# A hybrid decoder layer on one core: the MLP's up projection by Strassen's seven block products

## The chip, the cores and the metric

The kernel runs on one core of a Trainium2 chip. The metric is the device time of one execution in microseconds (us); less is better. The engines named below are PE (matrix products and transposes), DVE (vector engine), ACT (scalar engine), POOL (GpSimd) and SP, which here only issues transfers. Each engine runs its own list of instructions in order and waits, instruction by instruction, for what the others produce.

## The reference

One decoder layer on 512 tokens of 1024 channels, in fp32. Two mixers (HGRN2 and native sparse attention) read the same normalised input; then come the parts that matter here:

```python
merged = (jax.nn.sigmoid(ga) * (y_a @ w_branch_a[i])
          + jax.nn.sigmoid(gb) * (y_b @ w_branch_b[i]))
h = h + rms_norm(merged @ w_out[i], norm_post_mix[i])
v = rms_norm(h, norm_pre_mlp[i])
ff = jnp.square(jax.nn.relu(v @ w_up[i])) @ w_down[i]
h = h + rms_norm(ff, norm_post_mlp[i])
e = (p[i] @ w_ple[i]) * jax.nn.sigmoid(h @ w_ple_gate[i])
h = h + rms_norm(e, norm_ple[i])
```

`w_up` is 1024 x 4096, `w_down` 4096 x 1024, the branch weights, `w_out` and `w_ple_gate` are 1024 x 1024, and `w_ple` is 256 x 1024. A projection must be nearly as exact as in fp32.

## The kernel before

**Products in three parts.** Each fp32 operand is split into a high part, which ACT makes by a cast to the reduced type fp32r, and a low part, which is the rest and which DVE makes by a subtraction (`split`, lines 60 and 61). A product is then three matmuls, high by high, high by low and low by high, added in PSUM (the accumulator banks that PE writes). The order of instructions on each engine is set by a scheduler at build time.

**Weights.** `weights` (line 89) lets SP load 512 KB into a `raw` tile of 128 x 1024, ACT cast it into `whi`, and DVE subtract for `wlo`. There are three `raw` tiles and six pairs of `whi` and `wlo` from the merge on, in two pools that take turns.

**Stages.** Up to about 685 us stand the input norm, the projections, the attention and HGRN2; their order of instructions is the same before and after. The merge (lines 824 to 868) computes 16 tiles of 128 channels, in turns of branch a and branch b, and gates them into `ta` and `tb`. `w_out` follows token tile by token tile (`proj_n`, line 886, `acc` tiles in PSUM). Its function `evac_o` (lines 924 to 941) takes each of four tiles of 128 tokens through: sum of squares (ACT, `sqs`), product with the norm's weights (DVE, `facc`), reciprocal root (`rsa` and `rsb` on DVE, `rsr` on POOL), residual with `x` into `h1` (listed as `h`; DVE), a second sum of squares and norm into `vn` (DVE), and transposes of `vn` by PE into two PSUM banks named `tr`, from which ACT and DVE make `vh` and `vl`, the operand of the up projection. `h1` stays on chip.

**MLP.** In four quarters of 1024 columns of `w_up`, the up projection has eight tiles of 128 columns each. The weights stand still in PE and 512 tokens of `vh` and `vl` move through: 8 x 3 matmuls of 512 columns for a tile. The first four tiles of quarter 0 are done in halves of 256 tokens (`up_mm`, line 963), tokens 0 to 255 first. `up_evac` applies Relu and Square (ACT) and splits into `fh` and `fl`. After each quarter `proj_n` multiplies these with 1024 rows of `w_down` into `facc`. At the end come `w_ple`, the last quarter of `w_down` with its residual, `w_ple_gate` and the output.

Of the kernel before, what the change touches and what calls it, by code (L numbers as in the profile page):

```python
# [7 lines left out]
FT = mybir.dt.float32  # L8
FR = mybir.dt.float32r
# [10 lines left out]
NT = 4  # L20
# [8 lines left out]
def hybrid_layer(ctx: ExitStack, tc: tile.TileContext, x, p, w_in, w_branch_a, w_branch_b, w_out,  # L29
# [33 lines left out]
    # Main-stream matmuls recorded in `rec` are placed in TensorE's order behind the  # L63
    # marked ones of another stream, spread evenly along it.
# [1029 lines left out]
```

## Time and profile before

| | |
|---|---|
| Median of 3 runs | 1259.81 us (1258.06 to 1261.55) |
| Span of the profiled execution | 1257.9 us (first to last instruction) |
| Mean granted clock of PE | 0.992 of full speed |
| PE busy | 1217.4 us (97%) |
| DVE busy | 710.5 us (56%) |
| ACT busy | 589.3 us (47%) |
| POOL busy | 171.0 us (14%) |
| HBM read, written | 107.54 MB, 10.49 MB |

The profile is of one execution. Its own time is known as the span only: what lies around the first and last instruction is not part of it, and the medians of runs are times of the whole execution. Matmuls are pipelined, so a row's duration of one (0.28 or 0.40 us) is longer than the distance from one start to the next. The granted clock is 1.00 at the upper of PE's two levels (2.4 GHz) and 0.50 at the lower (1.2 GHz); a value between is a mean over a stretch that holds both.

### The profile page before, as it was taken

The page shows a single profiled execution, that of the slowest core. Times are in us where ns is not written, and L with a number is a line of the kernel's source. Part 1 is how long each engine was busy: PE and PEld are TensorE (multiplying, and loading weights), DVE is VectorE, ACT ScalarE, POOL GpSimd, SP SyncE. Part 2 cuts the span into 40 slices and gives each one's busy share as a digit, 9 for nine tenths or more (in the row PEclk, how much of TensorE's full clock was granted, in tenths as well). Part 3 has the DMA queues.
Part 4 walks back from the last instruction along what each step waited for, and adds up shares of the span by engine and source line. Part 5 has one row for each costly group of instructions (what it writes and reads, how often), then busy time and mean ns, then how long its engine had stood idle before and what let it go on. Part 6 is the DMA issues. An engine that isn't in the chain of part 4 may idle for free. (4 is left out here: it accounts for less than half of the span.)

```text
span 1257.9 us, 17684 instructions
## 1 busy us (share of the span) xinstructions
PE 1217.4 (97%) x6719; PEld 1023.5 (81%) x6719; DVE 710.5 (56%) x1354; ACT 589.3 (47%) x1213; POOL 171.0 (14%) x281
## 2 busy tenths in 40 slices
PE   7999999999999999999999999999999999999997
PEld 6888877778777899999978678888888888888885
DVE  6765687757787376767684445374233242342564
ACT  6455676756777334434343222355344143144242
POOL 2022432433321101110100111010000000000000
PEclk9999998999999999999999999999999999999999
DMA  6335221221112523131324854344333242243211
GB/s 181 109 109 166 61 54 38 54 65 43 52 42 68 168 68 84 52 85 51 85 76 125 227 165 170 97 113 126 84 101 100 67 118 84 67 151 100 68 51 67
DMA packets 145095, 119.18 MB, mean 95 GB/s; under 512 B 8257, under 2 KB 123889, under 8 KB 145010
## 3 DMA queue, kind: packets, MB, share of 16 engines
q1 hardware_dynamic: 135008, 101.20, 28.3%
q0 software_dynamic: 3200, 10.49, 2.8%
q10 hardware_dynamic: 6802, 6.36, 1.6%
q8 instruction: 53, 0.87, 0.3%
q14 instruction: 32, 0.26, 0.1%
HBM read 107.54 MB, written 10.49 MB: 94 GB/s over the span
## 5 line engine op out<-in xcount | busy, mean ns | idle before, releaser
L61 DVE TENSOR_TENSOR wlo<-raw,whi 128x1024 fp32r<-128x1024 f32 (+1 forms) x157 | 192.3, 1226 | 218.2 <-ACT whi L60 217.9
L60 ACT CAST whi<-raw 128x1024 fp32r<-128x1024 f32 (+1 forms) x175 | 182.8, 1046 | 261.6 <-PE acc L896 77.1
L122 PE MATMUL ps<-whi,uh 128*128 128x256 f32 (+1 forms) x512 | 148.0, 290 | 1.5 <-DVE kcd L246 0.5
L124 PE MATMUL ps<-whi,ul 128*128 128x256 f32 (+1 forms) x512 | 146.7, 287 | 0.0
L123 PE MATMUL ps<-wlo,uh 128*128 128x256 f32 (+1 forms) x512 | 146.4, 286 | 0.2 <-DVE wlo L61 0.2
L82 PE MATMUL ps<-uh,whi 128*128 128x512 f32 x288 | 118.2, 410 | 0.0
L84 PE MATMUL ps<-uh,wlo 128*128 128x512 f32 x288 | 114.7, 398 | 0.3 <-DVE wlo L61 0.3
L83 PE MATMUL ps<-ul,whi 128*128 128x512 f32 x288 | 114.7, 398 | 0.0
L82 PE MATMUL up<-vh,whi 128*128 128x512 f32 (+1 forms) x288 | 105.9, 370 | 1.4 <-ACT vh L60 1.4
L83 PE MATMUL up<-vl,whi 128*128 128x512 f32 (+1 forms) x288 | 106.0, 369 | 0.1
L84 PE MATMUL up<-vh,wlo 128*128 128x512 f32 (+1 forms) x288 | 105.7, 368 | 0.0
L894 PE MATMUL acc<-whi,fh 128*128 128x512 f32 x256 | 101.4, 396 | 0.0
L896 PE MATMUL acc<-whi,fl 128*128 128x512 f32 x256 | 100.3, 394 | 0.0
L122 PEld LDWEIGHTS ps<-whi,uh 128*128 128x128 f32 x512 | 96.8, 189 | 4.3 <-PE cps L84 0.7
L895 PE MATMUL acc<-wlo,fh 128*128 128x512 f32 x256 | 100.1, 391 | 0.0
L123 PEld LDWEIGHTS ps<-wlo,uh 128*128 128x128 f32 x512 | 96.9, 189 | 1.3 <-DVE wlo L61 0.5
L124 PEld LDWEIGHTS ps<-whi,ul 128*128 128x128 f32 x512 | 96.8, 189 | 0.6 <-issue 0.2
L458 ACT ACTIVATE P<-ps_s,nm 128x128 f32<-128x128 f32 (+3 forms) x128 | 67.7, 530 | 28.4 <-DVE nm L456 26.0
L456 DVE TENSOR_REDUCE nm<-ps_s 128x1 f32<-128x128 f32 (+3 forms) x128 | 61.3, 484 | 27.4 <-PE ps_s L454 26.7
L61 DVE TENSOR_TENSOR ptl<-tr,pth 128x512 fp32r<-128x512 f32 x82 | 55.6, 684 | 26.5 <-ACT pth L60 26.3
L84 PEld LDWEIGHTS ps<-uh,wlo 128*128 128x128 f32 x288 | 54.1, 188 | 12.5 <-DVE wlo L61 0.4
L82 PEld LDWEIGHTS up<-vh,whi 128*128 128x128 f32 x288 | 53.8, 188 | 11.3 <-ACT vh L60 1.9
(283 smaller groups left out, 2554.2 us busy)
## 6 DMA issues: line engine op xcount, KB each, us to landing
raw<-in_w_in_dram SPq DMA_DIRECT2D x58, 512.0 KB, 3.8
raw<-in_w_up_dram SPq DMA_DIRECT2D x32, 512.0 KB, 4.4
raw<-in_w_down_dram SPq DMA_DIRECT2D x32, 512.0 KB, 3.7
raw<-in_w_in_dram SPq DMA_DIRECT2D x17, 256.0 KB, 3.5
raw<-in_w_branch_a_dram SPq DMA_DIRECT2D x8, 512.0 KB, 5.3
raw<-in_w_branch_b_dram SPq DMA_DIRECT2D x32, 128.0 KB, 4.0
raw<-in_w_out_dram SPq DMA_DIRECT2D x8, 512.0 KB, 4.0
raw<-in_w_ple_gate_dram SPq DMA_DIRECT2D x8, 512.0 KB, 3.8
```

The costliest lines, as they stand in the source:

```text
L60: act.copy(hi, src)
L61: (lo_eng or dve).tensor_sub(lo, src, hi)
L82: rec.append(pe.matmul(ps, lh, rh, start=first, stop=False).ins)
L83: pe.matmul(ps, lh, rl, start=False, stop=False)
L84: pe.matmul(ps, ll, rh, start=False, stop=last)
L122: rec.append(pe.matmul(o, stat[0][:, k, s], hi[:, i], start=(k == 0), stop=False).ins)
L123: pe.matmul(o, stat[0][:, k, s], lo[:, i], start=False, stop=False)
L124: pe.matmul(o, stat[1][:, k, s], hi[:, i], start=False, stop=(k == NK - 1))
L458: act.activation(pt[:, :nk], ps[:, :nk], AF.Exp, bias=nm, accum_out=sums[:, h:h + 1])
L894: pe.matmul(ps, stat[0][:, k, s], hi[:, k % 2], start=(k == 0), stop=False)
L895: pe.matmul(ps, stat[0][:, k, s], lo[:, k % 2], start=False, stop=False)
L896: pe.matmul(ps, stat[1][:, k, s], hi[:, k % 2], start=False, stop=(k == nk - 1))
```

## The change

The activations of the up projection, transposed, are cut into 2 x 2 blocks: two halves of the 1024 channels (the summed index) by two halves of the 512 tokens. So is each group of 512 columns of `w_up`: two halves of the channels by two of 256 columns. Eight groups make up the 4096 columns. Instead of the eight block products of such a group, seven are computed, in Strassen's scheme in Winograd's form, from sums and differences of blocks: A11, A12, A22 and S1 to S4 on the side of the activations, made once by `to_forms`, and three blocks as loaded, or four differences, on the side of the weights, made by DVE for every group. Each product keeps the split in three matmuls: 2 tiles of 128 columns x 4 x 128 channels x 3 matmuls of 256 tokens. Results that several outputs share are kept in one PSUM bank `X`, which goes on accumulating through A11, S2, S1 and S4, and copied out between by ACT (`side`); DVE adds the rest. `finish` applies Relu, Square and the split to a 256 x 256 block of the result. The products of neighbouring groups are started in an interleaved order (`steps`).

`vn` has one buffer. `h1` is computed in place of the loaded `x` tile, stored to DRAM by SP, and loaded again for the residual after the MLP. The `raw` tiles become six (2 and 4, in turns 0, 1, 1), the pairs stay 3 and 3. `w_post2` and the copies of `w_ple` are placed in other buffers. The core of the diff:

```diff
+    turn = {"raw": [0], "pair": [0]}
+    RAWS, PAIRS = (2, 4), (3, 3)
...
-        wpool.append(wtx)
+        wpool.append(wty)
+        turn["raw"], turn["pair"] = [0, 1, 1], [0, 1]
...
-            residual(wo, halves(facc[:, t]), sss[t], 4 * EPS, xt, h1[:, t])
+            residual(wo, halves(facc[:, t]), sss[t], 4 * EPS, xt, xt)
...
-            vn = wo.tile([128, D], FT, name="vn")
+            vn = wo.tile([128, D], FT, name="vn", bufs=1)
...
-            to_t(vn, t, vh, vl)
+            sp.dma_start(h1_d[t], xt)
+            to_forms(vn, t)
+
+        def to_forms(vn, t):
+            s = (slice(None), slice(None), slice(t % 2 * 128, t % 2 * 128 + 128))
+
+            def into(form, src):
+                split(form[0][s], form[1][s], src)
+
+            ps = [transpose4(tp, [vn[:, (4 * g + i) * 128:(4 * g + i + 1) * 128] for i in range(4)])
+                  .rearrange("p (k t) -> p k t", k=4) for g in range(2)]
...
+            if t < 2:
+                for form, q, f in ((A11, ps[0], f0), (A12, ps[1], f1)):
+                    into(form, q)
+                    act.copy(f, q)
+                return
...
+            act.copy(f0, ps[0])
+            dve.tensor_add(f1, f0, ps[1])
+            into(A22, ps[1])
+            dve.tensor_sub(f0, g0, f0)
+            dve.tensor_sub(g0, f1, g0)
+            into(S2, g0)
+            into(S3, f0)
+            into(S1, f1)
+            dve.tensor_sub(g1, g1, g0)
+            into(S4, g1)
...
-            for i, (wt, ps) in enumerate(held):
-                up_mm(ps, wt, 256, 512)
-                up_evac(early - len(held) + i, ps)
-            for m in range(early, 8):
-                wt = w_simple(w_up, 0, NK, (qd * 8 + m) * 128, 128)
-                ps = tp.tile([128, 512], FT, name="up", tag="up", bufs=3)
-                up_mm(ps, wt, 0, 512)
-                up_evac(m, ps)
...
+        b11 = block(0, 0)
+        X = bank("up", 3)
+        product(X, pair_of(b11, 4, 256), A11, True)
+        m1 = side(X)
+        yield
+        b21 = block(1, 0)
+        Z = bank("tr", 2)
+        product(Z, pair_of(b21, 4, 256), A12, True, True)
+        dve.tensor_add(m1, m1, Z)
+        finish(m1, g, 0, 0)
+        b12, b22 = block(0, 1), block(1, 1)
+        dve.tensor_sub(b11, b12, b11)
+        t2 = raw_tile().rearrange("p (a b) -> p a b", a=4)
+        dve.tensor_sub(t2, b22, b11)
+        product(X, pair_of(t2, 4, 256), S2, False)
+        u2 = side(X)
+        dve.tensor_sub(b12, b22, b12)
+        Y = bank("up", 3)
+        product(Y, pair_of(b12, 4, 256), S3, True)
+        product(X, pair_of(b11, 4, 256), S1, False)
+        w = side(X)
+        dve.tensor_add(w, w, Y)
+        finish(w, g, 1, 1)
+        yield
+        product(X, pair_of(b22, 4, 256), S4, False, True)
+        finish(X, g, 1, 0)
+        dve.tensor_sub(b21, b21, t2)
+        product(Y, pair_of(b21, 4, 256), A22, False, True)
+        dve.tensor_add(u2, u2, Y)
+        finish(u2, g, 0, 1)
+        yield
+
+    groups = [up_group(g) for g in range(8)]
+
+    steps = [(0, 1)]
+    for g in range(8):
+        steps += [(g, 2)] + ([(g + 1, 1)] if g < 7 else []) + [(g, 3)]
...
+        if c == 1:
+            h1 = endp.tile([128, D], FT, name="h1", bufs=2)
+            sp.dma_start(h1, h1_d[t])
+            residual(ff, halves(facc[:, t]), ssf[t], EPS, h1, facc[:, t])
+            to_t(facc[:, t], t, vh2, vl2)
```

The scheduler's order moves with it. On PE, at the hand-over from `w_out` to the up projection, these rows stood before (`tr<-ident,vn` are the transposes of the token tiles 2 and 3, `tr<-ident,raw` those of p, and `up` rows the halves of the first up tiles):

```order
L82 MATMUL up<-vh,whi 128x256
L147 MATMUL tr<-ident,vn 128x128 x4
L83 MATMUL up<-vl,whi 128x256
L84 MATMUL up<-vh,wlo 128x256
L147 MATMUL tr<-ident,vn 128x128 x4
L82 MATMUL up<-vh,whi 128x256
...
L83 MATMUL up<-vl,whi 128x256
L84 MATMUL up<-vh,wlo 128x256
L147 MATMUL tr<-ident,vn 128x128 x8
L82 MATMUL up<-vh,whi 128x256 x3
L147 MATMUL tr<-ident,raw 128x128 x4
```

And now, from the end of the product with A11 to the first of S3 and, for the next group, of A11 (the `tr<-a12h` rows are the product with A12, whose result lies in a bank of the transposes):

```order
L1010 MATMUL up<-a11h,whi 128x256
L1010 MATMUL up<-a11l,whi 128x256
L1010 MATMUL up<-a11h,wlo 128x256
L158 MATMUL tr<-ident,vn 128x128 x16
L158 MATMUL tr<-ident,raw 128x128 x8
L1010 MATMUL tr<-a12h,whi 128x256
...
L1010 MATMUL tr<-a12l,whi 128x256
L1010 MATMUL tr<-a12h,wlo 128x256
L1010 MATMUL up<-s3h,whi 128x256
L1010 MATMUL up<-a11h,whi 128x256
L1010 MATMUL up<-a11l,whi 128x256
L1010 MATMUL up<-a11h,wlo 128x256
```

Before, up matmuls stood between the transposes of tile 2, tile 3 and p; now all these transposes stand in a row behind A11's product and ahead of A12's.

On DVE, the same place before, from the last product of `w_out` with the norm's weights (`facc<-acc,w_post`) to the last parts of `vl`:

```order
L928 TENSOR_TENSOR facc<-acc,w_post 128x512
L911 SCALAR_TENSOR_TENSOR rsb<-ssz,rsa 128x1
L61 TENSOR_TENSOR wlo<-raw,whi 128x1024
L918 SCALAR_TENSOR_TENSOR h_8006<-facc,rsr,xt 128x512 x2
L61 TENSOR_TENSOR wlo<-raw,whi 128x1024
L61 TENSOR_TENSOR vl<-tr,vh 128x4x128
L910 TENSOR_SCALAR rsa<-ssh 128x1
L61 TENSOR_TENSOR vl<-tr,vh 128x4x128
L911 SCALAR_TENSOR_TENSOR rsb<-ssh,rsa 128x1
L940 SCALAR_TENSOR_TENSOR vn<-h_8006,rsr,w_pre 128x512 x2
L61 TENSOR_TENSOR vl<-tr,vh 128x4x128 x2
```

And now, from tile 2's `vn` and tile 3's residual (`xt<-facc,rsr,xt`) to tile 3's lo part of A22 (`a22l`; `raw<-raw` is a difference of weight blocks):

```order
L958 SCALAR_TENSOR_TENSOR vn<-xt,rsr,w_pre 128x512 x2
L936 SCALAR_TENSOR_TENSOR xt<-facc,rsr,xt 128x512 x2
L1048 TENSOR_TENSOR raw<-raw 128x1024
...
L983 TENSOR_TENSOR facc<-facc 128x512
L61 TENSOR_TENSOR s1l<-facc,s1h 128x4x128
L980 TENSOR_TENSOR facc<-facc,tr 128x512
L61 TENSOR_TENSOR s3l<-facc,s3h 128x4x128
L987 TENSOR_TENSOR facc<-facc 128x512
L61 TENSOR_TENSOR s2l<-facc,s2h 128x4x128
L61 TENSOR_TENSOR ptl<-tr,pth 128x512
L982 TENSOR_TENSOR facc<-facc 128x512
L61 TENSOR_TENSOR a22l<-tr,a22h 128x4x128
```

Between the norm of tile 2 and that of tile 3 a difference of weight blocks came in, and behind it, in place of four lo parts of `vl`, the sums and lo parts of the forms, in which those of tiles 2 and 3 and of p alternate.

On SP, the loads of the merge before (a branch b tile of 512 KB is four loads of 128 KB; `ybl` is its operand, eight loads):

```order
L96 DMA raw<-in_w_branch_a_dram 128x8x128 x2
L96 DMA raw<-in_w_branch_b_dram 64x4x128 x4
L96 DMA raw<-in_w_branch_a_dram 128x8x128
L851 DMA ybl<-yl_d 128x512 x8
L96 DMA raw<-in_w_branch_a_dram 128x8x128
L96 DMA raw<-in_w_branch_b_dram 64x4x128 x4
L96 DMA raw<-in_w_branch_a_dram 128x8x128 x2
L96 DMA raw<-in_w_branch_b_dram 64x4x128 x4
L96 DMA raw<-in_w_branch_a_dram 128x8x128
L96 DMA raw<-in_w_branch_b_dram 64x4x128 x4
```

And now:

```order
L112 DMA raw<-in_w_branch_a_dram 128x8x128 x2
L112 DMA raw<-in_w_branch_b_dram 64x4x128 x8
L112 DMA raw<-in_w_branch_a_dram 128x8x128
L863 DMA ybl<-yl_d 128x512 x8
L112 DMA raw<-in_w_branch_a_dram 128x8x128 x2
L112 DMA raw<-in_w_branch_b_dram 64x4x128 x12
L112 DMA raw<-in_w_branch_a_dram 128x8x128 x3
```

Loads of later tiles moved forward past those of the tiles between, and a second branch b tile is asked for ahead of `ybl`.

## Rows read from the trace of the kernel before

**Rows 1.** The page, busy time, share of the span and instructions of PE.
```profile
PE 1217.4 (97%) x6719; PEld 1023.5 (81%) x6719; DVE 710.5 (56%) x1354; ACT 589.3 (47%) x1213; POOL 171.0 (14%) x281
```

**Rows 2.** Windows of hand-over and MLP: busy us by engine, PEclk, DMA share, GB/s.
```profile
818.00:865.00 47.00, 43.99 (x300) 39.71 (x299) 29.58 (x49) 26.94 (x48) 6.14 (x8) 1.00 0.43 124
865.00:1256.00 391.00, 385.20 (x1683) 312.87 (x1681) 147.43 (x180) 143.34 (x211) 4.92 (x9) 1.00 0.30 89
```

**Rows 3.** Timeline of PE, single matmuls: start us, duration us, line, operands, tile.
```profile
849.35 0.28 PE L82 MATMUL up<-vh,whi 128*128 128x256 f32 x1
...
851.71 0.28 PE L82 MATMUL up<-vh,whi 128*128 128x256 f32 x1
...
858.07 0.39 PE L82 MATMUL up<-vh,whi 128*128 128x512 f32 x1
...
864.34 0.40 PE L82 MATMUL up<-vh,whi 128*128 128x512 f32 x1
...
1249.80 0.40 PE L896 MATMUL acc<-whi,vl 128*128 128x512 f32 x1
```

**Rows 4.** Waits of PE from 800 us to the end: total us, times, longest.
```profile
PE up L82 <- ACT vh L60: 1.4, 1, 1.4
PE tr L147 <- DVE vn L940: 1.3, 1, 1.3
```

**Rows 5.** Lines by form, PE, 825 to 1150 us: count, busy us, mean ns, idle.
```profile
L82 PE MATMUL up<-vh,whi 128*128 128x512 f32 x224 | 88.3, 394 | 0.0
...
L82 PE MATMUL up<-vh,whi 128*128 128x256 f32 x64 | 17.5, 285 | 1.4 <-ACT vh L60 1.4
```

**Rows 6.** Lines by form, DVE and ACT, 865 to 1250 us, same columns.
```profile
L61 DVE TENSOR_TENSOR wlo<-raw,whi 128x1024 fp32r<-128x1024 f32 x64 | 78.2, 1224 | 137.5 <-ACT whi L60 137.3
L61 DVE TENSOR_TENSOR fl<-r,fh 128x512 fp32r<-128x512 f32 x28 | 19.4, 692 | 20.3 <-ACT fh L60 20.3
...
L60 ACT CAST whi<-raw 128x1024 fp32r<-128x1024 f32 x63 | 66.0, 1049 | 146.6 <-PE acc L896 75.4 <-PE up L83 56.9 <-DMA raw<-in_w_up_dram 14.0
L970 ACT ACTIVATE r<-r 128x512 f32<-128x512 f32 x28 | 17.7, 633 | 0.9
...
L969 ACT ACTIVATE r<-up 128x512 f32<-128x512 f32 x28 | 16.6, 592 | 6.2 <-PE up L84 6.2
...
L996 ACT COPY facc<-acc 128x512 f32<-128x512 f32 x8 | 4.7, 587 | 28.1 <-PE acc L896 28.1
```

**Rows 7.** Timeline of the hand-over: PE, DVE and ACT.
```profile
827.45 1.03 PE L147 MATMUL tr<-ident,vn 128*128 128x128 f32 x8
...
839.52 0.15 DVE L911 SCALAR_TENSOR_TENSOR rsb<-ssh,rsa 128x1 f32<-128x1 f32 x1
840.39 1.41 DVE L940 SCALAR_TENSOR_TENSOR vn<-h,rsr,w_pre 128x512 f32<-128x512 f32 x2 [0.72 <-POOL rsr L912]
...
827.89 0.63 ACT L904 ACTIVATE sqs<-h 128x512 f32<-128x512 f32 x1 [1.97 <-DVE h L918]
```

**Rows 8.** Windows in attention, merge and hand-over, columns as in rows 2.
```profile
208.00:212.00 4.00, 3.98 (x19) 2.93 (x19) 2.90 (x9) 1.98 (x7) 0.48 (x1) 0.50 0.09 16
700.00:715.00 15.00, 14.62 (x64) 11.62 (x62) 7.07 (x9) 4.62 (x5) 1.10 (x2) 1.00 1.00 248
742.00:746.00 4.00, 4.00 (x11) 3.13 (x12) 2.36 (x3) 0.00 (x0) 0.55 (x1) 0.57 0.63 151
828.00:832.00 4.00, 2.49 (x19) 2.05 (x18) 3.95 (x9) 3.82 (x9) 1.06 (x2) 1.00 0.81 222
```

**Rows 9.** Waits in the merge, 680 to 830 us (PE) and 695 to 746 us.
```profile
PE ps L82 <- DVE ta L861: 3.1, 3, 2.1
PE ps L82 <- DVE tb L861: 2.0, 1, 2.0
...
ACT whi L60 <- DMA raw<-in_w_branch_b_dram: 21.6, 5, 5.7
```

**Rows 10.** DMA issues, 780 to 845 us: count, KB each, median us to landing.
```profile
raw<-in_w_up_dram SPq DMA_DIRECT2D x8, 512.0 KB, 4.2
```

More of the change, by code (lines that the diff above doesn't have):

```diff
@@ L868, in hybrid_layer @@
     yt_pool.release()
+    yb_hi.release()
+    yb_pool.release()
     tp = ctx.enter_context(tc.tile_pool(name="tp", reuse_waits="tile", bufs=2, space=PSUM))
-    vh = yb_hi.tile([128, NK, 512], FR, name="vh", tag="yh")
-    vl = yb_pool.tile([128, NK, 512], FR, name="vl", tag="yl")
+    af = tc.alloc_tile_pool(name="af", reuse_waits="tile", bufs=1, side="right")
+    A11, A12, A22, S1, S2, S3, S4 = (
+        tuple(af.tile([128, 4, 256], FR, name=f"{n}{e}") for e in "hl")
+        for n in ("a11", "a12", "a22", "s1", "s2", "s3", "s4"))
     def row(pool_, w, name, r=None):
@@ L951, in hybrid_layer @@
+    ptl = ff.tile([128, 2, 512], FR, name="ptl", bufs=1)
     for i in range(2):
@@ L1040, in hybrid_layer, with product @@
-    pq.release()
-    wpool[1].release()
-    yb_hi.release()
+    w_post2 = row(ff, norm_post_mlp, "w_post2")
+    ssf = [ff.tile([128, 2], FT, name=f"ssf{t}", bufs=1) for t in range(NT)]
+    fbuf = {}
+    def product(ps, wt, form, first, last=False):
+        for c in range(2):
+            for k in range(4):
+                f, e = first and c == 0 and k == 0, last and k == 3
+                cs = slice(c * 128, c * 128 + 128)
+                for n, (l, r) in enumerate(((wt[0], form[0]), (wt[0], form[1]), (wt[1], form[0]))):
+                    pe.matmul(ps[:, c], l[:, k, cs], r[:, k], start=f and n == 0,
+                              stop=e and n == 2, skip_group_check=True)
@@ new lines, in hybrid_layer, with up_to, down @@
+    groups = [up_group(g) for g in range(8)]
+    steps = [(0, 1)]
+    for g in range(8):
+        steps += [(g, 2)] + ([(g + 1, 1)] if g < 7 else []) + [(g, 3)]
+    done = {}
+    def up_to(g):
+        while done.get(g) != 3:
+            i, n = steps.pop(0)
+            next(groups[i])
+            done[i] = n
+    def down(qd, evac):
+        w = w_down[qd * 1024:(qd + 1) * 1024]
+        for c in range(2):
+            ch = [w_simple(w, kk * 128, 2, c * 512, 512) for kk in range(0, NK, 2)]
+            for t in range(NT):
+                ps = tp.tile([128, 512], FT, name="acc", tag="acc", bufs=3)
+                s = slice(t * 128, t * 128 + 128)
+                for k in range(NK):
+                    hi, lo = ch[k // 2]
+                    fh, fl = fbuf[2 * qd + k // 4]
+                    pe.matmul(ps, fh[:, k % 4, s], hi[:, k % 2], start=(k == 0), stop=False)
+                    pe.matmul(ps, fh[:, k % 4, s], lo[:, k % 2], start=False, stop=False)
+                    pe.matmul(ps, fl[:, k % 4, s], hi[:, k % 2], start=False, stop=(k == NK - 1))
+                evac(c, t, ps)
@@ new lines, in hybrid_layer, with evac_d @@
+    for qd in range(3):
+        up_to(2 * qd + 1)
+        def evac_d(c, t, ps, qd=qd):
+            d = facc[:, t, c * 512:c * 512 + 512]
+            if qd == 0:
+                act.copy(d, ps)
+            else:
+                dve.tensor_add(d, ps, d)
+        down(qd, evac_d)
+    up_to(7)
+    af.release()
+    endp = tc.alloc_tile_pool(name="endp", reuse_waits="tile", bufs=1, side="right")
+    vh2 = endp.tile([128, NK, 512], FR, name="vh2")
+    vl2 = endp.tile([128, NK, 512], FR, name="vl2")
```

172 lines of the change are left out of this document (82 added, 90 removed).

## The prediction

> **What bounds the kernel now.** I read the busy shares first. PE, the matrix engine, works 1217.4 us of a span of 1257.9 us [rows 1], so any microsecond of matrix work that is really taken away counts, and any wait that is added counts as well. By stretch [rows 2] the MLP (from 865 us on) is PE alone: 385.20 busy of 391.00 us at full clock, with DVE (the vector engine) at 147.43 and ACT (the scalar engine) at 143.34, under 40% each. The rest after that is the chain behind the last matmul, which starts at 1249.80 [rows 3] and which the change leaves as it is. In the 47 us before, where w_out hands over to the up projection, PE is busy 43.99 us. The waits of PE from 800 us to the end are two only: 1.4 us for ACT's cast of vh and 1.3 us for vn [rows 4]; in the whole MLP behind them there is none. So the change can win by fewer columns, and can lose where the new up projection waits for its operands.
>
> **1. Columns.** Before, the up projection has 3 x 224 = 672 matmuls of 512 columns and 3 x 64 = 192 of 256 [rows 5] (the lines of the other two parts have the same counts). Their cadence is read from starts [rows 3]: 849.35 to 851.71 is 20 steps of 256 columns, 0.118 us each; 858.07 to 864.34 is 27 steps of 512, 0.2322 us each. So the up projection costs 672 x 0.2322 + 192 x 0.118 = 156.0 + 22.7 = 178.7 us. After, each of 8 groups does 7 products of 2 x 4 x 3 = 24 matmuls of 256 columns, 1344 in all (the order has 480 matmuls more, which is 1344 - 864, so the eighth product is really gone). They cost 1344 x 0.118 = 158.6 us: **-20.1 us**. All stationary tiles change with each matmul before and after, and the 256-column rows already run so, so no hidden price is left in the shorter shape. The Trainium skill ("TensorE: Matmul & The Clock Gate", section "Wait — 56ns, not 53.3ns?") gives start to start N / 2.4 GHz plus about 2.5 ns. By that the estimate would be 215.8 and 109.2 ns, and a gain of 19.2 us; the trace here shows 232 and 118 ns, so the rows decide.
>
> **2. The load of the other engines in the up phases.** A group of 512 columns gives PE 168 x 0.118 = 19.8 us. DVE gets 7 lo parts and 4 subtractions of the same 128x1024 shape (the subtraction was not there before; both are two-input operations on that shape, so I take the same 1.22 us), and 3 additions and 4 lo parts of 512 elements at 0.69 [rows 6]: 13.4 + 4.8 = 18.2 us, against 4 x (1.22 + 0.69) = 7.6 before. ACT gets 7 casts at 1.05, 4 times Relu, Square and a cast of the result (0.592 + 0.633, and about 0.62 for the cast), and 3 copies at 0.587: 16.5 us [rows 6]. DVE is thus 92% as loaded as PE within a group. But two groups are followed by 192 matmuls of a down quarter (44.6 us of PE), in which DVE has only 8 casts' lo parts and 8 additions (15.3 us), and the order lets the pairs of the next group be made there. Over two groups and a down quarter PE has 84.2 us and DVE 51.7. I therefore take **0**, from 0 up to +8 (2 us in each of four phases). A gain is excluded, as no wait is there now.
>
> **3. Hand-over from w_out to the up projection.** This is where the change costs. Before, PE runs halves of up tiles on tokens 0 to 255 while tokens 256 to 511 are still normalised, which leaves 2.7 us of waits [rows 4]. After, only the product with A11 needs tokens 0 to 255 alone; A12's product stands behind all transposes on PE (the order on PE), and S1 to S4 need all tokens. I walked the order with the durations of [rows 6, 7]. The w_out's last tile ends at 827.45, where the transposes of vn begin [rows 7]. ACT then does two sums of squares with two weight casts between, the sum of squares of tile 3, and two copies that free the transpose banks (0.63 + 1.05 + 0.63 + 1.05 + 0.63 + 2 x 0.587, begun at 827.89 before): vn of tile 1 is transposed at about 830.5 to 831.7, and its lo part comes on DVE behind two weight lo parts and the product with w_post, at about 833.3. PE waits about 4.6. A11 takes 2.8 us, and ends at 836.1; vn of tile 2 is transposed at 836.5. Tile 3 still needs its residual (1.4), a subtraction of weight blocks that stands between (1.2), the sum of squares (1.4), POOL's power (DVE's rsb at 839.52, its vn at 840.39 before, so 0.9), in which a weight lo part fits, and vn (1.41 for both halves): PE has its first half at 841.4 (wait 3.8), and the second only when DVE has read the bank of tile 2, at 843.9 (wait 1.9). The transposes of p need the next bank, which is free once DVE has done tile 3's lo part of A22, at about 849.8: on DVE nine operations of 0.69 and less stand from 843.9 to there (the order on DVE; wait 4.7). Then A12 runs, and S2's operand is there at 854.4 (wait 0.6 more, with the 0.4 ahead of tile 2). Waits together: 4.6 + 0.4 + 3.8 + 1.9 + 4.7 + 0.6 = 16.0 us, less 2.7 = **+13.3 us**. The bounds: +3 if banks and casts come free sooner than the walk has it (PE would then wait about twice as long as now), +18 if the load of x for tile 2 is late too: its buffer now waits for the store of h1, and a load of 512 KB takes 4.2 us to land [rows 10].
>
> **4. Clock.** The granted clock falls behind some waits: it is 0.57 in 742 to 746, right behind the merge's longest wait of 2.1 us, and 0.50 through 208 to 212 in the attention, but 1.00 in 828 to 832, where the wait of 1.4 us lies [rows 4, 8, 9]. With waits of 4 to 5 us I count on 1.2 GHz for A11 or A12 (2.8 us each, so as much again), partly inside the next wait: **+2.5 us** (0 to +5).
>
> **5. Merge.** PE waits there for ta and tb, 3.1 + 2.0 = 5.1 us; behind it ACT's cast waits 21.6 us in all for loads of w_branch_b, five times [rows 9]: loads of the next tile start only when one of three raw buffers is free. The low clock after it costs 4 x 0.43 = 1.7 us [rows 8]. With 2 + 4 raw buffers, SP (the queue that issues loads) asks for tiles further ahead (the order on SP). In 700 to 715, though, the DMA is at 1.00 and 248 GB/s [rows 8], so part of the lateness is plain transfer. I take two thirds of 6.8: **-4.5 us** (0 to -6.8).
>
> **6. h1 through DRAM and the end.** The four stores and four loads of 512 KB are 4 MB over 450 us; a load takes 4.2 us [rows 10], and the reloads are issued a down tile or more ahead of their use. Cover: PE's down matmuls; without it, 4 us. The copies of w_ple and the last stage stay. I take 0.
>
> Sum against the profiled execution: 1257.9 - 20.1 + 0 + 13.3 + 2.5 - 4.5 = 1249.1 us of span. The median is 1.9 us above that span, so the forecast is **1251.0 us**.
>
> **Rivals.** (a) *The hand-over is covered*: PE's queue finds work, or ACT and DVE run through the forms quicker; then terms 3 and 4 fall to about 0 to 3, and the time is about 1236. For it: DVE is busy 29.58 of 47 us now [rows 2], so slack exists. Against it: the order is fixed, and the named operations stand in a row. (b) *DVE binds in the up phases*: 18.2 against 19.8 us leaves 1.6 us a group; if groups lose 1 us each, the time is 1259. For it, the subtractions for a group stand in a row before its casts; against it, the down quarters between. (c) *Slower*: one bank X takes A11, S2, S1 and S4 in turn, and ACT must copy it out between (3 times a group, 24 in all). The copy is 0.59 us, and 22 or more other matmuls (2.6 us) mostly stand between. If ACT is in two casts and a Relu-Square-cast first, the copy ends 2.1 + 1.8 + 0.6 = 4.5 us after, and PE waits 1.9; on all 24 that is +46. It decides (slower) from 0.5 us on average (12.6 / 24); I price it at 0.8, +19, 1270. (d) *The clock*: every burst between two waits of the hand-over starts at 1.2 GHz, so the PE work there (transposes 4.6, A11 2.8, A12 2.8, the first of S3 and A11 0.6, so 10.8 us) counts twice: +10.8 in place of +2.5, 1259.3. This is what the Trainium skill describes (same page, section "HAM oscillation — how this bites in real kernels"): short bursts between waits each begin at the low clock; the rows at 0.57 and 1.00 above bear it out only in part. That the change would not do what it says is excluded by the matmul count.
>
> **Numbers.** Forecast 0.50 (its own range 1245 to 1257), (a) 0.17, (b) 0.12, (d) 0.08, (c) 0.13. A measurement of this kernel can tell about 0.3%, 3.8 us, from no change. Faster than 1256: the forecast's most, (a), and a share of (b): 0.69. Within: 0.18. Slower: (c), 0.13. The range reaches down to (a)'s middle and up over (b) and (d): 1237 to 1263, which leaves out half of (a) and (c).
>
> **What would show it.** Up matmuls of 256 columns x1344 at a cadence of 0.118; waits of PE of about 16 us between 825 and 856, by DVE's forms and the transposes, and none over 2 us in the later up phases; a clock of 0.5 to 0.8 in one or two slices there; waits in the merge under 2 us. The prediction is wrong if PE waits for copies called side, or for wlo, in each group (b, c), or if the hand-over costs under 5 us (a).

## The result and the profile after

The changed kernel takes 1250.51 us in the median of five runs (1248.81 to 1251.59), the kernel before 1258.06 us in the five runs beside them (1255.41 to 1261.55). The ratio is 0.9934 with an interval of [0.9917, 0.9951]: faster by 0.5 to 0.8%. The profiled execution of the changed kernel has a span of 1247.7 us and took 1249.47 us, so the time around the span is 1.8 us.

The page's line of busy times, answering to [rows 1]:

```profile
PE 1199.2 (96%) x7199; PEld 1031.9 (83%) x7199; DVE 794.2 (64%) x1448; ACT 629.9 (50%) x1273; POOL 169.4 (14%) x281
```

PE does 18 us less work in a span that is 10 us shorter, and DVE 84 us more. Where the time went is read from starts of matmuls in the two timelines of PE:

| From the start of ... to the start of ... | before | after | difference |
|---|---|---|---|
| the span, to the first matmul of the merge | 685.17 | 684.19 | -0.98 |
| that, to the first matmul of w_out (the merge) | 97.04 | 91.47 | -5.57 |
| w_out, first to last matmul | 45.01 | 45.01 | 0.00 |
| that, to the first matmul with w_down (the hand-over and the first up products) | 53.05 | 58.13 | +5.08 |
| that, to the last matmul of all (the rest of the MLP, to w_ple_gate) | 369.53 | 360.77 | -8.76 |
| that, to the end of the span | 8.1 | 8.1 | 0.0 |

The waits of PE from 680 us on, where [rows 4, 9] stood (total, times, longest):

```profile
PE tr L158 <- DVE vn L958: 3.7, 1, 3.7
PE tr L158 <- DVE ptl L61: 3.1, 1, 3.1
PE up L1010 <- DVE a11l L61: 2.0, 1, 2.0
PE acc L912 <- ACT pw L1126: 1.5, 1, 1.5
PE tr L158 <- ACT facc L975: 1.3, 1, 1.3
PE ps L82 <- DVE ta L873: 1.1, 2, 0.9
PE up L1010 <- ACT side L1034: 0.8, 1, 0.8
PE tr L158 <- ACT facc L979: 0.7, 1, 0.7
PE ps L82 <- DVE tb L873: 0.3, 1, 0.3
```

The first lines in order of time are `facc` (L975) 1.3, `a11l` 2.0, `vn` 3.7, `facc` (L979) 0.7 and `ptl` 3.1: 10.7 us at the hand-over, between 821 and 843 us. `ta` and `tb`, 5.1 us before, are 1.4 us now. Two waits are new in the MLP: 0.8 us for a copy `side`, once, and 1.5 us for a copy of w_ple's result.

Windows of the hand-over's waits and of the MLP behind them, columns as in [rows 2]:

```profile
828.00:860.00 32.00, 24.36 (x165) 22.55 (x164) 28.75 (x40) 17.75 (x30) 1.08 (x2) 0.75 0.23 73
860.00:1242.00 382.00, 377.65 (x2236) 331.87 (x2234) 213.84 (x250) 181.37 (x266) 4.32 (x8) 1.00 0.32 101
```

From 828 to 860 us DVE is busy 28.75 of 32.00 us and PE 24.36, at a mean clock of 0.75. From 860 us on PE is busy 377.65 of 382.00 us: the up phases run without DVE in their way, though DVE works 213.84 us there.

DVE's timeline at the hand-over (start, duration, line, operands), seven of its rows:

```profile
822.31 2.35 DVE L61 TENSOR_TENSOR wlo<-raw,whi 128x1024 fp32r<-128x1024 f32 x2
...
825.31 0.68 DVE L61 TENSOR_TENSOR a11l<-tr,a11h 128x512 fp32r<-128x512 f32 x1
...
831.14 1.22 DVE L1048 TENSOR_TENSOR raw<-raw 128x1024 f32<-128x1024 f32 x1
...
835.56 0.68 DVE L980 TENSOR_TENSOR facc<-facc,tr 128x512 f32<-128x512 f32 x1
...
837.36 0.69 DVE L61 TENSOR_TENSOR a22l<-tr,a22h 128x512 fp32r<-128x512 f32 x1 [0.39 <-ACT a22h L60]
...
842.77 0.68 DVE L61 TENSOR_TENSOR a22l<-tr,a22h 128x512 fp32r<-128x512 f32 x1
...
846.97 0.68 DVE L61 TENSOR_TENSOR s2l<-facc,s2h 128x512 fp32r<-128x512 f32 x1
```

Two lo parts of weights (822.31) stand ahead of `a11l` (825.31), for which PE waits; the difference of weight blocks stands at 831.14, the first sum of the forms at 835.56, tile 2's `a22l` at 837.36, tile 3's at 842.77 and the last lo part at 846.97. From 835.56 to there it is a row of 19 operations, most of them 0.60 us from start to start.

The clock, windows of 4 us:

```profile
824.00:828.00 4.00, 2.05 (x12) 1.95 (x12) 3.25 (x7) 1.96 (x4) 1.08 (x2) 0.84 1.05 352
828.00:832.00 4.00, 3.43 (x22) 3.19 (x20) 4.00 (x6) 1.61 (x5) 0.00 (x0) 0.74 0.07 22
832.00:836.00 4.00, 0.88 (x4) 0.71 (x4) 3.50 (x7) 1.54 (x4) 1.08 (x2) 0.69 0.65 226
836.00:840.00 4.00, 2.44 (x9) 1.43 (x8) 3.57 (x7) 3.72 (x8) 0.00 (x0) 0.50 0.11 36
840.00:844.00 4.00, 1.61 (x6) 1.21 (x7) 4.00 (x8) 2.72 (x5) 0.00 (x0) 0.50 0.00 0
844.00:848.00 4.00, 4.00 (x24) 4.00 (x24) 4.00 (x8) 1.28 (x3) 0.00 (x0) 0.60 0.45 131
848.00:852.00 4.00, 4.00 (x37) 4.00 (x36) 4.00 (x5) 2.43 (x4) 0.00 (x0) 1.00 0.02 4
```

It is under 1.00 from 824 to 848, at the lower level (1.2 GHz) through 836 to 844, and back at 848. In PE's timeline the product with A12 stands in that stretch:

```profile
843.50 0.58 PE L1010 MATMUL tr<-a12h,whi 128*128 128x256 f32 x1
...
844.10 0.41 PE L1010 MATMUL tr<-a12h,wlo 128*128 128x256 f32 x1
...
846.87 0.41 PE L1010 MATMUL tr<-a12h,whi 128*128 128x256 f32 x1
```

It begins at 843.50, when DVE's `a22l` of 842.77 is done, and from 844.10 to 846.87 its 13 steps take 0.213 us each.

Lines by form after 860 us: the subtraction of weight blocks, which no row of before showed, and ACT's copy of the bank `X`:

```profile
L1048 DVE TENSOR_TENSOR raw<-raw 128x1024 f32<-128x1024 f32 x6 | 7.4, 1225 | 9.3 <-DMA raw<-in_w_up_dram 9.3
...
L1034 ACT COPY side<-up 128x512 f32<-128x512 f32 x22 | 12.7, 580 | 0.0
```

The subtraction takes the 1.22 us that were assumed, the copy 580 ns.

### The profile page after: what moved, and what is told of

Same layout as the page of the kernel before. It is cut to its first block, busy times and chain, and to the rows that moved or that the text cites. A ratio compares the mean times of both kernels' runs of the same rounds, so it can differ in the third digit from the quotient of the medians.

```text
span 1247.7 us, 18829 instructions
## 1 busy us (share of the span) xinstructions
PE 1199.2 (96%) x7199; PEld 1031.9 (83%) x7199; DVE 794.2 (64%) x1448; ACT 629.9 (50%) x1273; POOL 169.4 (14%) x281
## 5 line engine op out<-in xcount | busy, mean ns | idle before, releaser
L60 ACT CAST whi<-raw 128x1024 fp32r<-128x1024 f32 (+1 forms) x199 | 207.7, 1046 | 216.3 <-PE acc L1094 61.7
L61 DVE TENSOR_TENSOR wlo<-raw,whi 128x1024 fp32r<-128x1024 f32 (+1 forms) x181 | 220.9, 1224 | 140.1 <-ACT whi L60 139.6
L83 PEld LDWEIGHTS ps<-ul,whi 128*128 128x128 f32 x288 | 54.2, 188 | 10.2
L82 PEld LDWEIGHTS ps<-uh,whi 128*128 128x128 f32 x288 | 54.2, 188 | 10.0
L1092 PEld LDWEIGHTS acc<-whi,fh 128*128 128x128 f32 x256 | 48.1, 188 | 11.3
L1093 PEld LDWEIGHTS acc<-wlo,fh 128*128 128x128 f32 x256 | 48.3, 189 | 11.0
```

Of the source, the lines that this page charges most:

```text
L60: act.copy(hi, src)
L61: (lo_eng or dve).tensor_sub(lo, src, hi)
L82: rec.append(pe.matmul(ps, lh, rh, start=first, stop=False).ins)
L83: pe.matmul(ps, lh, rl, start=False, stop=False)
L1092: pe.matmul(ps, fh[:, k % 4, s], hi[:, k % 2], start=(k == 0), stop=False)
L1093: pe.matmul(ps, fh[:, k % 4, s], lo[:, k % 2], start=False, stop=False)
```

## Experiments

All times are medians; each kernel ran on a chip beside the kernel before, and the ratios are to that.

**e1: three raw tiles in the merge.**

```diff
-    RAWS, PAIRS = (2, 4), (3, 3)
+    RAWS, PAIRS = (2, 3, 1), (3, 3)
...
-        wpool.append(wty)
-        turn["raw"], turn["pair"] = [0, 1, 1], [0, 1]
+        wpool.extend((wty, wtz))
+        turn["raw"], turn["pair"] = [0, 2], [0, 1]
...
+    turn["raw"] = [0, 1, 1, 0, 1, 2]
     ff = tc.alloc_tile_pool(name="ff", reuse_waits="tile", bufs=2)
```

> The change with one part undone: in the merge and in w_out only three raw tiles take turns (two and one), as before; from the MLP on there are six. Theory (the raw tiles are what made the merge 5.6 us shorter in the trace of the change): PE's waits for ta and tb in the merge come back to about 4 to 6 us, the low clock behind them too, and the time rises by 4 to 7 us, to about 1255 to 1257. Rival (the merge gained by the new order or place of buffers, or by chance): waits in the merge stay under 2 us and the time is within 2 us of the change.

Measured: 1253.54 us against 1257.42, ratio 0.9969 [0.9957, 0.9981], so 4.4 us above the change by the ratios (0.9969 - 0.9934, of 1258). The merge takes 96.03 us from its first matmul to that of w_out, 4.56 more than in the change. Waits in the merge, of PE, and of ACT for branch b:

```profile
PE ps L82 <- DVE ta L874: 2.8, 2, 2.3
PE ps L82 <- DVE tb L874: 1.6, 1, 1.6
...
ACT whi L60 <- DMA raw<-in_w_branch_b_dram: 23.2, 5, 5.6
```

The waits for late loads of branch b are back (23.2 us on ACT; 21.6 before [rows 9], 6.1 in the change), and with them 4.4 us on PE. The theory holds: the additional raw tiles are worth 4.6 us of the merge's 5.6.

**e2: no sums of activation blocks.** S1 to S4 are not made; their products take A21 or A22. The number of matmuls and the weight side are the change's.

```diff
-            act.copy(f0, ps[0])
-            dve.tensor_add(f1, f0, ps[1])
+            into(S3, ps[0])
             into(A22, ps[1])
-            dve.tensor_sub(f0, g0, f0)
-            dve.tensor_sub(g0, f1, g0)
-            into(S2, g0)
...
-        product(X, pair_of(t2, 4, 256), S2, False)
+        product(X, pair_of(t2, 4, 256), S3, False)
```

> Leaves out the sums and differences on the side of the activations: S1 to S4 are not made, and their products use the third block S3 (set to A21) or A22 instead, with the same number of matmuls and the same weight blocks; the output is not the layer's. Theory (DVE's row of sums and lo parts makes PE wait at the hand-over for the transposes' bank): the wait for ptl of 3.1 us and most of the 0.7 go, the clock is back earlier, and the time falls by 4 to 8 us, to 1243 to 1247. Rival (the waits are those of the norm's own chain, residual, sum of squares and vn): only 0 to 2 us less.

Measured: 1246.67 us against 1257.42, ratio 0.9910 [0.9890, 0.9931]: 3.0 us below the change by the ratios, under the theory's 4 to 8; in the profiles the time from w_out's last matmul to the first down matmul falls from 58.13 to 53.26 us. The longest wait at the hand-over:

```profile
PE tr L158 <- DVE s3l L61: 4.8, 1, 4.8
```

The wait for `ptl` is gone, but 4.8 us stand where 3.7 and 0.7 stood, ahead of tile 3's transposes: DVE's vn of tile 3 starts at 836.57 there, and the lo part that frees tile 2's bank comes behind it. So DVE's row of forms is one part of the loss, and the chain of the norm ahead of it, with weight blocks in between, is the other. Neither theory alone is right.

**e3: p later.**

```diff
-    pn = raw_tile().rearrange("p (t c) -> p t c", t=NT)
-    sp.dma_start(pn, p.rearrange("(t q) c -> q t c", q=128))
...
         up_to(2 * qd + 1)
+        if qd == 0:
+            load_p()
```

> One move: p is loaded, transposed and split after the first two groups of the up projection, not ahead of them. Theory (transposes of p stand in a row behind DVE's forms, and A12's product behind them): the wait of 3.1 us for their bank goes, A12's product runs in that time, and the time falls by 3 to 5 us with the clock. Rival (PE then waits for S2 or S3 for as long, since DVE is the engine that is behind): 0 to 1 us less.

Measured: 1249.74 us against 1257.42, ratio 0.9931 [0.9909, 0.9952]: 0.4 us below the change, which its interval cannot tell from nothing. The profiled execution took 1255.18 us (the other four 1247.98 to 1250.37) and has a wait of 4.7 us for `ta` in the merge that no other profile here shows; its hand-over, to the first down matmul, is 56.53 us, 1.6 shorter. In size the rival is nearer: the transposes of p were not what held PE. The waits that it named, for S2 or S3, are not in the list, though; 1.0 us for tile 3's lo part of A22 and 1.0 us for a cast of weights stand there instead.

**e4: cover for PE.** p later, the product with A12 of groups 0 and 1 in a bank of w_out, A11 of group 1 earlier.

```diff
-        Z = bank("tr", 2)
+        Z = bank(*(("acc", 3) if g < 2 else ("tr", 2)))
...
-    steps = [(0, 1)]
+    steps = [(0, 1), (1, 1)]
     for g in range(8):
-        steps += [(g, 2)] + ([(g + 1, 1)] if g < 7 else []) + [(g, 3)]
+        steps += [(g, 2)] + ([(g + 1, 1)] if 0 < g < 7 else []) + [(g, 3)]
```

> Three moves: p later as in the run before; the product with A12 of the first two groups goes to the banks that w_out has left (acc), not to a bank of the transposes; and A11's product of group 1 is issued ahead of A12's of group 0. So 96 matmuls (11.3 us at the full clock) that need tokens 0 to 255 alone stand among the transposes of tiles 2 and 3. Theory (PE waits at the hand-over, 10.7 us, and the low clock behind them, about 5 us, are a matter of cover): the waits fall to 2 to 4 us, the clock stays over 0.9 and the time falls by 8 to 13 us, to 1238 to 1243. Rival (DVE is the bound of the hand-over; the lo parts of three more weight pairs ahead of the forms push S2 and S3 back by 3 to 4 us): 3 to 6 us less, and waits for s2 or s3 of 4 us and more.

Measured: 1255.77 us against 1257.42, ratio 0.9982 [0.9972, 0.9992]: 6 us slower than the change. That is worse than both expectations. The three longest waits of PE at the hand-over:

```profile
PE up L1012 <- ACT s2h L60: 3.3, 1, 3.3
PE up L1012 <- DVE a11l L61: 2.9, 1, 2.9
PE acc L1012 <- DVE wlo L61: 2.5, 1, 2.5
```

The waits sum to 14.2 us with the smaller ones, 3.5 more than in the change, though 96 matmuls now stand among the transposes, where the change has 24 (the scheduler put those of p at 847.84 and 850.41 all the same, ahead of S3's product, and PE waits 2.0 us there). DVE's timeline says why:

```profile
823.31 1.22 DVE L1065 TENSOR_TENSOR raw<-raw 128x1024 f32<-128x1024 f32 x1
824.44 2.35 DVE L61 TENSOR_TENSOR wlo<-raw,whi 128x1024 fp32r<-128x1024 f32 x2
826.72 0.68 DVE L61 TENSOR_TENSOR a11l<-tr,a11h 128x512 fp32r<-128x512 f32 x1
...
846.11 1.22 DVE L1052 TENSOR_TENSOR raw<-raw 128x1024 f32<-128x1024 f32 x1
```

A difference of weight blocks for a later step (823.31) now stands ahead of `a11l` beside the two lo parts, and more weight work among the forms (846.11 is one piece), so that from the first sum (835.37) to tile 3's lo part of S2 (857.25) DVE takes 21.9 us, where the change takes 11.4. What covers PE must first be made by DVE, and DVE was the engine behind. The theory of cover falls for cover of this kind; DVE's work ahead of each operand is what counts.

**e5: all eight products.** Blocks A11, A12, A21 (in S3) and A22, no sums on either side. The edit does not move p, though the expectation says so: it is transposed at the hand-over, as in the change.

```diff
+        product(X, p11, A11, True)
+        product(X, p21, A12, False, True)
+        finish(X, g, 0, 0)
...
+        product(X, p12, S3, True)
+        product(X, p22, A22, False, True)
+        finish(X, g, 1, 1)
```

> The change's layout with all eight block products in place of seven: blocks A11, A12, A21 and A22 of the activations, no sums on either side, four weight pairs a group, 8 x 24 matmuls of 256 columns; p is loaded later, six raw tiles as in the change. Theory (term 1: the seven products save 8 x 24 x 0.118 = 22.7 us of columns, and about 16 us of waits and low clock at the hand-over eat most of it): the MLP from the first down product on takes longer by the columns, the hand-over has under 4 us of waits and a clock near 1.00, and the whole is 1258 to 1264, 8 to 13 us over the change. Rival (the gain is the merge's alone, and Strassen's scheme is worth nothing net): 1249 to 1254.

Measured: 1258.40 us against 1258.92, ratio 1.0001 [0.9991, 1.0010]: 8.4 us above the change by the ratios. The waits of PE at the hand-over are two, 1.9 us for `a11h` and 1.5 for `a11l`. From the first down matmul to the last matmul it takes 372.18 us, the change 360.77, for 120 matmuls more: with the change's waits of 0.8 and 1.5 us taken off, 13.7 / 120 = 0.114 us each. So the theory holds on both sides: by term 1's count the eighth product costs 22.7 us, and 8.4 of them are left, since e5's hand-over is so much shorter. Without the scheme the new layout is no faster than the kernel before: what its merge gains (6.1 us in the profiles), its two short waits, its low clock behind them and its 1536 matmuls of 256 columns take (hand-over and MLP are 4.8 us longer).

**e6 and e7: forms on POOL.** Five lo parts and two subtractions of the forms go to POOL; in e7 also the lo parts of the first weight block of groups 0 and 1.

```diff
-            into(S2, g0)
-            into(S3, f0)
-            into(S1, f1)
-            dve.tensor_sub(g1, g1, g0)
-            into(S4, g1)
+            lo = pool if t == 2 else None
+            into(S2, g0, lo)
+            into(S3, f0, lo)
+            into(S1, f1, lo)
+            pool.tensor_tensor(g1, g1, g0, op=OP.subtract)
+            into(S4, g1, pool)
```

> p later as in e3, and of the work on the forms 4 lo parts of tile 2, 2 subtractions and tile 3's lo part of S4 go to POOL, which is idle there, in place of DVE. Theory (DVE's row of operations bounds the hand-over, as it is busy without a break from 815 to 848 in the change's trace; POOL takes about 1.3 us where DVE takes 0.6 from start to start): DVE's row is 7 x 0.6 = 4.2 us shorter, S2's and S3's operands are there 2 to 4 us sooner, and the time falls by 2 to 5 us below the change, to 1245 to 1248. Rival (POOL is too slow, and S2 waits for it): within 1.5 us of e3 or above it.

> As e6, and the lo parts of the first weight block of groups 0 and 1 (2.4 us each on POOL, 1.2 on DVE) go to POOL as well. Theory: A11's product and vn of tile 2 come 1 to 2 us sooner, and the time falls by 0 to 3 us more. Rival (the powers of the norm stand behind these on POOL and the norm's chain is late): 0 to 3 us above e6.

Measured: e6 1252.11 us against 1258.92, ratio 0.9949 [0.9933, 0.9964]; e7 1249.80, ratio 0.9934 [0.9919, 0.9949]. Neither is below the change, and their hand-overs are 56.28 and 56.30 us, as e3's 56.53. The profiles show nothing of the 2.3 us between the two medians at the hand-over, and what e7's theory names did not come: A11's second matmul starts 7.3 us behind w_out's last, in e6 6.5. (DVE's row is not without a break in the change's trace, as e6's expectation has it: the window 824 to 828 above has DVE at 3.25 of 4.00 us.) A reason is in e6's timelines, of POOL:

```profile
842.99 1.72 POOL L988 TENSOR_TENSOR facc<-facc 128x512 f32<-128x512 f32 x1
844.68 1.75 POOL L61 TENSOR_TENSOR s2l<-facc,s2h 128x512 fp32r<-128x512 f32 x1
...
848.08 1.74 POOL L988 TENSOR_TENSOR facc<-facc 128x512 f32<-128x512 f32 x1
```

and of DVE:

```profile
840.60 0.68 DVE L983 TENSOR_TENSOR facc<-facc 128x512 f32<-128x512 f32 x1
...
843.50 1.77 DVE L983 TENSOR_TENSOR facc<-facc 128x512 f32<-128x512 f32 x1
...
848.59 0.67 DVE L1048 TENSOR_TENSOR side<-side,tr 128x512 f32<-128x512 f32 x1
```

At 840.60 DVE subtracts two tiles of on-chip memory in 0.68 us. While POOL subtracts, the same operation takes 1.77 us (843.50), and POOL 1.7 where I had reckoned 1.3. An addition of which one operand lies in PSUM (848.59) takes 0.67 us beside POOL's subtraction of 848.08. The Trainium skill says so ("SBUF — State Buffer", section "Who interferes with whom"): a DVE instruction with two inputs from on-chip memory contends with a POOL instruction that reads there, and one with at most one does not (outside modes that take both of DVE's ports). The trace agrees, with 1.77 against 0.67. Not every pair costs DVE: its subtraction of 841.20 keeps to 0.68 us beside one of POOL's that takes 1.86. But from 842.40 to 848.59 four of DVE's operations take 6.2 us where 2.4 were due, 3.8 of the 4.2 us that the move was to save.

**e8: filler matmuls.** The change with 36 matmuls whose result nothing reads.

```diff
+            if t >= 2:
+                fill = tp.tile([128, 512], FT, name="acc", tag="acc", bufs=3)
+                n = (24, 12)[t - 2]
+                for i in range(n):
+                    ins = pe.matmul(fill[:, 0:256], A11[0][:, i % 4, 0:128], A11[0][:, i % 4],
+                                    start=i == 0, stop=i == n - 1).ins
```

> The change with 24 matmuls of 256 columns behind the transposes of tile 2 and 12 behind those of tile 3, of A11 with itself, into a bank that nothing reads: they lie in waits of PE of 3.7 and 3.1 us and change no other work. Theory (term 4: waits lower the clock, and the clock costs about 5 us there, of which what lies inside DVE's row is hidden): the clock in 832 to 848 rises from 0.50 to 0.69 to over 0.8, the product with A12 after the waits runs at the full rate, and the time falls by 1 to 3 us. Rival (the clock costs nothing, since DVE's operands end the hand-over): within 0.7 us of the change. Third: the added matmuls delay the transposes and it is 1 to 3 us slower.

Measured: 1256.17 us against 1258.92, ratio 0.9980 [0.9968, 0.9993]: 5.8 us slower than the change. The longest wait of PE:

```profile
PE tr L160 <- DVE vn L960: 8.6, 1, 8.6
```

The wait for `vn` grew from 3.7 to 8.6 us. The filler takes a bank of w_out's, and w_out's last tile came behind it (its matmuls run from 832.17 to 837.50), and with it tile 3's norm. So more than the filler changed, and the run says nothing on the clock.

**e11: the filler moved.** Run last: the same filler, with its bank taken behind w_out's.

```diff
         proj_n(w_out, (mgh, mgl), NK, evac_o)
+        for t, n in ((2, 24), (3, 12)):
+            fill = tp.tile([128, 512], FT, name="acc", tag="acc", bufs=3)
+            for i in range(n):
+                ins = pe.matmul(fill[:, 0:256], A11[0][:, i % 4, 0:128], A11[0][:, i % 4],
+                                start=i == 0, stop=i == n - 1).ins
```

> The filler of e8 again, its bank taken behind all of w_out's, so that w_out's tiles keep their order: 24 matmuls of 256 columns behind the transposes of tile 2, 12 behind those of tile 3, whose result nothing reads. On DVE only a few operations behind the forms stand in another order. Theory (the clock costs about 2 us behind DVE's row, where the products with A12 and A11 run at half rate, and nothing within it): the waits of 3.7 and 3.1 us are filled in large part, the clock is at 1.00 when the row ends, and the time is 1 to 3 us below the change. Rival (the filler takes as long at the low clock as it hides, or delays the transposes): within 1 us of the change or above it.

Measured: 1249.33 us against 1258.86, ratio 0.9938 [0.9917, 0.9959]: the change's 0.9934 within the intervals. In the profiles w_out's end to the first down matmul is 56.98 us, 1.15 less than in the change. Windows, among them the two in which the change had 0.50 (836 to 844):

```profile
828.00:832.00 4.00, 4.00 (x21) 4.00 (x20) 3.70 (x5) 1.64 (x4) 0.00 (x0) 0.50 0.31 103
...
836.00:840.00 4.00, 3.20 (x24) 2.73 (x24) 3.93 (x7) 3.24 (x7) 0.00 (x0) 1.00 0.27 101
840.00:844.00 4.00, 1.04 (x5) 1.04 (x6) 4.00 (x8) 2.60 (x5) 0.00 (x0) 0.82 0.00 0
844.00:848.00 4.00, 4.00 (x28) 4.00 (x28) 3.92 (x8) 1.53 (x3) 0.00 (x0) 0.76 0.02 4
```

The clock is at 1.00 in 836 to 840 and at 0.82 behind, but at 0.50 in 828 to 832, where the change had 0.74, and the hand-over gains 1.15 us at most (its order behind the row is a little other, too). PE's busy time times what is missing of the clock, an estimate of what it costs, comes to 3.9 us from 824 to 848, against 5.1 in the change. With the clock up PE still waits in DVE's row, 3.0 us for S3's operand (until 842.96). In size the rival is nearer. That the clock costs nothing inside DVE's row is not shown, since the filler took away no more than 1.2 of the 5.1 us.

**e9: eight products for group 0 alone.** A21 lies in S4's place until group 0 is done; then the sums are made. p is loaded later as well, as in e3.

```diff
-            act.copy(f0, ps[0])
-            dve.tensor_add(f1, f0, ps[1])
-            into(A22, ps[1])
+            for form, q, f in ((S4, ps[0], f0), (A22, ps[1], f1)):
+                into(form, q)
+                act.copy(f, q)
...
+        for th, (lo_k, hi_k) in enumerate(((A11, A12), (S4, A22))):
...
+                finish(ps, g, ch, th)
+        for t in (2, 3):
+            sums(t)
...
-    groups = [up_group(g) for g in range(8)]
-    steps = [(0, 1)]
+    groups = [up_eight(0)] + [up_group(g) for g in range(1, 8)]
+    steps = [(0, 3), (1, 1)]
```

> Group 0 of the up projection takes all eight products (with A21 held in the place of S4), groups 1 to 7 take seven; the sums S1 to S4 are made while group 0 runs, and p is loaded later as in e3. The result is the layer's. Theory (the change's loss is the hand-over alone: DVE's row of forms ahead of products that need them, with 10.7 us of waits and about 5 us of low clock): as in e5, waits at the hand-over fall to about 3 to 4 us and the low clock to one short stretch, for 24 matmuls more (2.8 us): 4 to 8 us below the change, 1242 to 1246. Rival (the sums then bind in groups 0 and 1, where DVE has them besides the weight blocks): waits for s2 or s3 of 3 us and more in group 1, and 1247 to 1251.

Measured: 1241.56 us (1240.54 to 1244.81) against 1257.77, ratio 0.9875 [0.9854, 0.9896]: 7.4 us below the change by the ratios, 7.0 below e3, which moves p alone, and the fastest kernel of the study. The three longest waits of PE:

```profile
PE up L1020 <- DVE a11l L61: 2.1, 1, 2.1
PE acc L912 <- ACT pw L1156: 1.5, 1, 1.5
PE up L1020 <- ACT a11h L60: 1.3, 1, 1.3
```

The hand-over has 4.0 us of waits in place of 10.7: the 2.1 and 1.3, and 0.3 and 0.2 for the two parts of A21. Its windows:

```profile
824.00:828.00 4.00, 1.93 (x15) 1.73 (x16) 4.00 (x8) 2.07 (x6) 0.29 (x1) 1.00 0.56 169
828.00:832.00 4.00, 4.00 (x36) 4.00 (x36) 4.00 (x7) 0.59 (x1) 2.78 (x2) 1.00 0.00 0
```

From w_out's last matmul to the first down matmul it takes 48.26 us, 9.87 less than the change, with 24 matmuls more. The theory holds: with products whose operands need no sums in front, the sums are covered by PE's work, and the waits for S2 or S3 that the rival named did not come.

**e10: w_ple's copies shared.**

```diff
-           lambda c, t, ps: act.copy(pw[:, t, c * 512:c * 512 + 512], ps))
+           lambda c, t, ps: (act.copy if t % 2 else dve.tensor_copy)(
+               pw[:, t, c * 512:c * 512 + 512], ps))
```

> As e9, and the copies of w_ple's result out of PSUM are shared by ACT and DVE, tile by tile, where ACT makes all in the change (PE waits 1.5 us for them in every run of the new layout, none before). Theory: the wait goes, 1 to 1.5 us below e9. Rival (DVE is as late there as ACT): the same as e9 within 0.7 us.

Measured: 1243.24 us (1241.43 to 1246.83) against 1257.77, ratio 0.9886 [0.9865, 0.9906]. The wait for the copies is still there, 1.4 us, now for DVE. The rival holds: no gain. (Not every run of the new layout has that wait, as the expectation says: e5 has none.) The windows of e10's hand-over, for which order and waits of PE are those of e9:

```profile
824.00:828.00 4.00, 1.93 (x10) 1.74 (x9) 4.00 (x9) 1.91 (x6) 0.45 (x1) 0.70 0.51 154
828.00:832.00 4.00, 4.00 (x21) 4.00 (x21) 4.00 (x7) 0.59 (x1) 2.62 (x2) 0.50 0.00 0
```

Both kernels wait 1.3 and 2.1 us from 821 to 826. In e9 the clock stayed at 1.00; in e10 it fell to 0.50, and e10 took 51.12 us to the first down matmul where e9 took 48.26. So 2.86 us are the price of one such fall, with the same work.

## Why the prediction was right, and where its terms were off

The span fell by 10.2 us where 8.8 were forecast, and the median to 1250.51 where 1251.0 was. From w_out's end to the last matmul the forecast was -20.1 + 13.3 + 2.5 = -4.3, and -3.7 was measured. The terms behind it are these.

**Columns** (-20.1): about -19. The count holds, and so does the cadence (0.117 us from one start to the next in the mean behind 880 us). From the first matmul with w_down on, where DVE is not in the way, 576 matmuls of 512 columns became 1032 of 256: 12.0 us by term 1's cadences. PE took 8.8 us less, with 2.3 us of new waits, so 11.1 were saved. The matmuls with w_down, whose work is the same, took 1.2 us back: they step at 0.2329 us in the mean, 0.2313 before; why is not shown. Ahead of there 192 matmuls of 256 and 96 of 512 columns became 312 of 256, -8.1 us by the same cadences. With the waits and the clock below that gives -8.1 + 8.0 + 5.1 = +5.0, and +5.1 was measured. So the term is -11.1 - 8.1 = -19.2. By the Trainium skill's rule for the cadence ("TensorE: Matmul & The Clock Gate", section "Wait — 56ns, not 53.3ns?") the estimate was 19.2 as well. In the cadence itself the traces do not agree with that rule, with 117 ns against its 109.2.

**Hand-over and clock** (+13.3 and +2.5, together 15.8): +13.1 together, differently shared. The chain on DVE came as walked. From w_out's last matmul to the product with A12 the walk had 850.4 - 827.2 = 23.2 us (it starts 0.6 behind tile 3's lo part of A22, at 849.8, for the transposes of p); the trace has 843.50 - 820.67 = 22.8. The walk's first step does not follow from its own durations, which add up to 5.2 us and from 827.89 end at 833.1, where it goes on at 830.5; in the trace the transposes start 1.7 us behind w_out's last matmul, in the walk 3.3. In the trace nine of DVE's operations took 5.4 us (837.36 to 842.77, start to start) for 5.9, and the second transposes of p waited for `ptl`, not for tile 3's `a22l`; that was done at 843.45, just as A12's product could start. The waits of PE are 10.7 us where 16.0 stood: `facc` and `a11l` 3.3 (4.6 in the walk), tile 3's first half 3.7 (3.8), its second 0.7 (1.9), the bank 3.1 (4.7), the rest 0 (1.0). Less 2.7 that is +8.0. The clock takes more than forecast: PE's busy time times what is missing of the clock is 5.1 us from 824 to 848 (for 844 to 848, 4.00 x 0.40 = 1.6). Both are the same thing in part, since the slow transposes and A11 ran in time in which PE would else have waited for DVE; e11, with the clock up in 836 to 840, waits 3.0 us for S3's operand. How large that part is no run shows. What the low clock adds to A12's product is 4.6 us (843.50 to 848.09) less 24 x 0.118, so 1.8 us. Where PE is the bound, one fall costs 2.86 (e9 and e10).

What the prediction said of the cause was half of it. DVE's row of forms was named: e2 takes its sums away and wins 3.0 us. e4 adds cover and loses 6, because DVE gets more to do ahead of each operand, and e9, with the sums moved behind products on plain blocks, takes the waits to 4.0. Rival (a), cover, with DVE's 29.58 busy of 47 us as slack, was thus no way out as such: there is no slack on DVE at the places that matter. Rival (d) is refuted by its size: the bursts did run at the low clock, but that took 5.1 us and not 10.8.

**Up phases** (0): +2.3, one wait of 0.8 us for `side` and 1.5 us for the copies of w_ple. Rivals (b) and (c) are refuted by the waits: of 24 copies of the bank X one was late.

**Merge** (-4.5): -5.6, of which e1 gives 4.6 back with three raw tiles. **h1 and the end** (0): 8.1 us behind the last matmul, before and after. The 0.98 us ahead of the merge, where the order is the same, is scatter as far as the runs show: in the thirteen profiles this stretch takes from 683.93 to 686.07 us.

So the sum of the parts is -19.2 + 8.0 + 5.1 + 2.3 - 5.6 - 1.0 = -10.4, against -10.2 in the spans; behind the first matmul with w_down it closes by construction, since the 11.1 is what was left there. Waits 5.3 too high, the clock 2.6 too low, 0.9 less for the columns, 2.3 not foreseen in the up phases, and the merge with the stretch ahead of it 2.1 better than forecast: these cancel but for 1.6 us. The total is better than its terms, and that it came within 1.4 us of the span is in part luck.

## What to carry to other kernels

A scheme that saves matmuls by sums pays for them where the first sums are due: look at which engine makes the operands there, and count what stands ahead of each operand on that engine, not how busy it is on average. Let the first group do the plain products, and make the sums under its cover; here that cost 24 matmuls and gave 7 us (e9 against e3). More work for PE in the gap is no cover if the engine that is behind must first make its operands.

## What was not expected of the hardware

POOL's subtractions in on-chip memory slowed three of DVE's from 0.68 to 1.77 us each while they ran (e6), which took back most of what moving work off DVE was to save. And the clock after the same two waits, of 1.3 and 2.1 us, stayed at 1.00 in one kernel and fell to 0.50 in another with the same order there (e9, e10), at 2.86 us: the same wait has no fixed price.
